# Inverse query norms written to DRAM word by word, and another place for one attention chain

## The chip, the cores and the metric

The kernel runs on one core of a Trainium2 chip. The metric is the device time of one execution in microseconds (us). The kernel before took 2829.93 us, the median of three runs (2829.88 to 2833.13).

The engines are named as in the profile: PE multiplies matrices (PEld is its weight load), DVE is the vector engine, ACT the scalar engine, POOL the GpSimd engine, and SP issues every DMA of this kernel from one queue, in order. PSUM is the memory into which PE writes; SBUF holds the tiles; DRAM is outside.

## What is computed

A decoder trunk of two layers over 1024 positions and 1024 channels, in float32. Layer 0 is a gated delta rule with a feed-forward part and a gated per-layer embedding. From its result one shared K and V are projected. Layer 1 is stick-breaking attention over them with eight heads of 128 channels, then again a feed-forward part and an embedding. Only the attention is touched by the change:

```python
def sb_mixer(hn, k_sh, v_sh, w_q, q_norm, w_out):
    q = (hn @ w_q).reshape(b_, s_, SB_HEADS, SB_HEAD_DIM)
    q = (rms_norm(q, q_norm) * (SB_HEAD_DIM ** -0.5)).transpose(0, 2, 1, 3)
    o = stick_breaking(q, k_sh, v_sh)
    return o.transpose(0, 2, 1, 3).reshape(b_, s_, SB_WIDTH) @ w_out

# stick_breaking, for a block of queries t and all keys s < t:
    z = einsum('bhtd,bhsd->bhts', q, k)
    log_not = where(mask, log_sigmoid(-z), 0.0)
    suffix = cumsum(log_not, axis=3, reverse=True) - log_not
    wgt = exp(where(mask, log_sigmoid(z) + suffix, -inf))
    out = einsum('bhts,bhsd->bhtd', wgt, v)
```

The norm of a query is one number per position, 1/sqrt(mean(q*q) + eps). The kernel doesn't scale q by it; it scales the scores z instead.

## The kernel before

**One program, planned while it is built.** The work is written as many small generators. `Flow` (lines 83 to 257) keeps a model of the time of each engine and of the DMAs. At each point of its own clock it runs, among the generators that are ready, the one with the lowest key; among equal keys the one that was spawned first (line 233). Where none is ready it takes the next step of one long "fill", the dense products. The order in which generators issue instructions is the order in each engine's queue, and stays fixed when the program runs. All instructions pass through one helper, so the profile puts line 64 to all of them, and tiles are told apart by name. A `take` waits for a free buffer of a kind in the model, a `give` frees it. The model's prices (lines 114 to 221) fix the order only.

**The attention stage** (`attention`, line 1739) has two kinds of work. The dense part (`sb_dense`, line 1794) goes over the heads, and in each over K, V, Q of the first and then of the second half of the positions, 512 columns at a time. A dense product is 24 matmuls into an `mm` bank: every float32 product is made of three, of high and low parts (`mm3`, line 337). Then `sb_features` (line 1817) splits the result into high and low parts for the attention. For Q and K it also transposes it, sums the squares of each position on ACT into a `[128, 4]` tile (partition = position within 128, column = which 128), and takes the power -0.5 on POOL.

For K this tile, `rk`, is used as it is, one number per partition. For Q the numbers are needed along the columns of z, the same in all partitions. So the tile goes through DRAM: PE transposes it into a `z` bank, DVE copies the `[4, 128]` result into `rr`, SP writes that to the DRAM tensor `rD`, and SP loads it back as one row of 512 numbers, repeated over 128 partitions (`rw`). The load waits for the write to have landed.

**The chains.** For each head h and half T, `sb_chains(h, T)` (line 1875) spawns three generators: `front` (key 2), `back` (key 0) and `out` (key 1). They go over the blocks of 128 keys from the last one backwards: four blocks for T = 0, eight for T = 1, of which the first four cover 128, 256, 384 and 512 columns. A front waits until the features of its head and half are there, and takes one of two `c` accumulator banks, which the back gives free at its last block. For each block: three matmuls make z; DVE scales it by `rk` and `rw` (tile `zs`); three ACT functions and a DVE one make the softplus (tile `t`); POOL masks the diagonal block; DVE splits it into `sh` and `sl`; four matmuls with triangles accumulate the suffix in `c`; DVE subtracts it from `zs`; POOL masks; ACT takes the exponential; DVE splits it into `wh` and `wl`; three matmuls with V accumulate the output in `o`. There are 4 `zs`, 2 `t`, 4 `sh`, 4 `sl`, 2 `wh`, 2 `wl` tiles, and 2 `z` banks for chains and features together.

**The end of the stage.** When the dense part is done, the fill goes on with `out_first` (line 1221), the output projection of the first half. Its first two units, f = 0 and 1, are made together: heads k = 0 to 6 of both, then k = 7 of both, which needs the output of chain (7,0). When its tile `x` exists, a chain's output is copied and split straight into it by ACT and DVE (`spill`, line 1184); before that it goes to DRAM (`oD`) and is loaded back (`load_o`, line 1206). The projection of the second half comes in the next stage, `tail(1)`, and needs chain (7,1).

All chains are spawned at the start of the stage, in the order (0,0), (0,1), (1,0), ... (6,1), (7,0), (7,1). So where two chains ask for the same thing at the same moment, the earlier one of this list gets it.

Of the kernel before, what the change touches and what calls it, by code (L numbers as in the profile page):

```python
# [15 lines left out]
P = 128  # L16
# [3 lines left out]
H = 8  # L20
# [249 lines left out]
class Net:  # L270
# [1468 lines left out]
    def attention(self):  # L1739
        nc, io, tc, flow = self.nc, self.io, self.tc, self.flow  # L1740
        with ExitStack() as es:
            sp = es.enter_context(tc.tile_pool(name="as", bufs=2, reuse_waits="tile"))
            pp = es.enter_context(tc.tile_pool(name="ap", bufs=2, space=PSUM, reuse_waits="tile"))
            self.sp, self.pp, self.lead = sp, pp, 0.0
            self.banks = (pp, "c", 2)
            self.enames = ()
            self.kq = sp.tile([P, 1], F32, name="kq", bufs=1)
            nc.vector.tensor_scalar(self.kq, self.small[:, 1:2], self.small[:, 2:3], float(P) ** -0.5, op0=ALU.mult, op1=ALU.mult)
            self.junk = sp.tile([P, P], F32, name="ajunk", bufs=1)
            nc.scalar.preload_act_table_set("natural_log_exp_and_others")  # L1750
            self.ast = [{} for _ in range(H)]
            self.hdone = [0] * H

            def second():
                hs = {}

                def loads():
                    for k in range(NK):
                        yield from self.take("zs")
                        hs[k] = self.t(sp, "zs", bufs=4)  # L1760
                        nc.sync.dma_start(hs[k], self.hD[k][:, HW:])
                        flow.mark(("hs", k))
                        yield 0.7

                flow.spawn(loads(), 0)
                yield lambda: flow.done(("hs", 0))
                yield from self.normed(("n3", 1), self.r1, lambda k: hs[k], None, lambda: self.t(sp, "sh", bufs=4), "sh", lambda: self.give("zs"))

            flow.spawn(second(), 0)
            for h in range(H):  # L1770
                for T in range(2):
                    self.sb_chains(h, T)
            yield from self.sb_dense()
            flow.spawn(self.late(), 4)
            yield lambda: ("tile", ("ol", 1, 0)) in flow.at
            yield from self.out_first(1, self.hD, lambda: self.t(sp, "xt"))
            yield lambda: all(e in flow.at for e in ("loaded10", "loaded11", ("put", 1)))
            self.enames = ()
# [38 lines left out]
    def sb_features(self, n, h, hf, ps):  # L1817
        nc, sp, pp, flow, st = self.nc, self.sp, self.pp, self.flow, self.ast[h]
        yield from self.take("ev")
        yield  # L1820
        ev = self.t(sp, "ev")
        nc.scalar.copy(ev, ps)
        self.give("mm")
        a, b = (self.t(sp, n + p, dt=F32R, bufs=4 if n == "q" else 5) for p in "hl")
        st[n, hf] = (a, b)
        yield
        yield from self.take("z")
        pt = self.t(pp, "z")
        for c in range(4):
            nc.tensor.transpose(pt[:, c * P : (c + 1) * P], ev[:, c * P : (c + 1) * P], self.ident)  # L1830
        yield
        if n == "v":
            nc.scalar.copy(a, pt)
            yield
            nc.vector.tensor_tensor(b, pt, a.bitcast(F32), op=ALU.subtract)
            self.give("z", "ev")
            flow.mark(("ap", n, h, hf))
            return
        ms = self.t(sp, "ms" + n, (P, 4))
        for c in range(4):  # L1840
            nc.scalar.activation(self.junk, pt[:, c * P : (c + 1) * P], AF.Square, accum_out=ms[:, c : c + 1])
        self.give("z")
        src = ev
        if n == "k":
            nc.vector.tensor_scalar(ev, ev, self.kq, None, op0=ALU.mult)
        nc.vector.tensor_copy(a, ev)
        yield
        nc.vector.tensor_tensor(b, ev, a.bitcast(F32), op=ALU.subtract)
        yield
        self.give("ev")  # L1850
        nc.vector.tensor_scalar(ms, ms, 1.0 / P, EPS, op0=ALU.mult, op1=ALU.add)
        yield
        r = self.t(sp, "r" + n, (P, 4), bufs=4)
        nc.gpsimd.tensor_tensor(r, ms, self.nhalf[:, :4], op=ALU.pow)
        yield
        if n == "k":
            st["rk", hf] = r
            flow.mark(("ap", n, h, hf))
            return
        yield from self.take("z")  # L1860
        pr = self.t(pp, "z")
        nc.tensor.transpose(pr[:4, :P], r, self.ident)
        yield
        rr = self.t(sp, "rr", (4, P))
        nc.vector.tensor_copy(rr, pr[:4, :P])
        self.give("z")
        yield
        nc.sync.dma_start(self.rD[2 * h + hf], rr)
        yield
        rq = self.t(sp, "rw", bufs=3)  # L1870
        nc.sync.dma_start(rq, self.rD[2 * h + hf].rearrange("c p -> (c p)").unsqueeze(0).to_broadcast([P, HW]))
        st["rq", hf] = rq
        flow.mark(("ap", n, h, hf))
# [218 lines left out]
```

## Time and profile before

| what | value |
|---|---|
| median of three runs | 2829.93 us (2829.88 to 2833.13) |
| profiled execution, its own time | 2831.9 us |
| its span | 2830.2 us |
| PE busy | 2759.6 us (98%) |
| DVE busy | 2026.8 us (72%) |
| ACT busy | 1276.1 us (45%) |
| POOL busy | 881.6 us (31%) |
| writes `rD` | 16, of 2 KB, from 1537.8 to 1966.4 us |
| loads `rw` | 16, of 256 KB, from 1539.1 to 1967.6 us |
| SP's waits for a write `rD` to land | 18.7 us in 15 waits, longest 2.1 |

Times in rows count from the start of the span. A row of the instructions in order of time has start, length, engine, operation, out<-in, shapes, count, and in brackets the idle time of the engine before it with what ended it. Matmuls overlap, and their ends are modelled: the rate of PE is the distance between starts, not the length. "PEclk" is the clock that was granted, 1.00 for full speed. The attention stage runs from about 1537 to 2060 us of the span.

### The profile page before, as it was taken

The page shows a single profiled execution, that of the slowest core. Times are in us where ns is not written, and L with a number is a line of the kernel's source. Part 1 is how long each engine was busy: PE and PEld are TensorE (multiplying, and loading weights), DVE is VectorE, ACT ScalarE, POOL GpSimd, SP SyncE. Part 2 cuts the span into 40 slices and gives each one's busy share as a digit, 9 for nine tenths or more (in the row PEclk, how much of TensorE's full clock was granted, in tenths as well). Part 3 has the DMA queues.
Part 4 walks back from the last instruction along what each step waited for, and adds up shares of the span by engine and source line. Part 5 has one row for each costly group of instructions (what it writes and reads, how often), then busy time and mean ns, then how long its engine had stood idle before and what let it go on. Part 6 is the DMA issues. An engine that isn't in the chain of part 4 may idle for free.

```text
span 2830.2 us, 37782 instructions
## 1 busy us (share of the span) xinstructions
PE 2759.6 (98%) x13203; PEld 2271.2 (80%) x13203; DVE 2026.8 (72%) x3861; ACT 1276.1 (45%) x2567; POOL 881.6 (31%) x742
## 2 busy tenths in 40 slices
PE   8899999999999999999999999999999999999999
PEld 7687777888878888888877778887777888888777
DVE  7777787784685655477867888998796655557783
ACT  6646545553443433322345566666453333422241
POOL 0101110110056666543201222221027666734400
PEclk9999999999999999999999999999999999999999
DMA  4312221227624444587432111114524444477622
GB/s 144 130 60 78 68 73 63 77 84 247 218 79 157 145 151 149 198 313 305 152 129 95 49 46 64 60 46 160 178 91 143 155 143 155 152 287 284 266 97 104
DMA packets 165631, 395.89 MB, mean 140 GB/s; under 512 B 34048, under 2 KB 35392, under 8 KB 155968
## 3 DMA queue, kind: packets, MB, share of 16 engines
q1 hardware_dynamic: 165440, 393.48, 39.1%
q8 instruction: 104, 1.70, 0.3%
q14 instruction: 87, 0.71, 0.1%
HBM read 274.29 MB, written 119.11 MB: 139 GB/s over the span
## 4 chain that ended last, share of the span: by engine, by line
PE 74%; DVE 14%; ACT 2%; issue 2%; DMA 2%; POOL 1%; SPq 0%; POOLq 0%; DVEq 0%; ACTq 0%
PE dn L64 37%; PE mm L64 27%; PE tp L64 3%; PE z L64 2%; PE c L64 2%; PE o L64 2%; DVE yr L64 1%; DVE x L64 1%; DVE ca L64 1%; DVE wlo L64 1%; DVE xr L64 1%; DVE u L64 1%; DVE v L64 1%; DVE hx L64 1%; PE po L64 1%
## 5 line engine op out<-in xcount | busy, mean ns | idle before, releaser
L64 PE MATMUL mm<-x,whi 128*128 128x512 f32 x2880 | 951.2, 400 | 12.8 <-DVE x L64 7.9
L64 PEld LDWEIGHTS mm<-x,whi 128*128 128x128 f32 x2880 | 533.6, 189 | 115.0 <-DVE x L64 13.8
L64 PE MATMUL mm<-x,wlo 128*128 128x512 f32 x1440 | 573.7, 398 | 0.0
L64 PE MATMUL dn<-x,whi 128*128 128x512 f32 x1776 | 549.2, 390 | 2.1 <-DVE x L64 0.9
L64 POOL TENSOR_TENSOR wlo<-raw,whi 128x512 fp32r<-128x512 f32 x236 | 346.0, 1487 | 442.0 <-ACT whi L64 368.1
L64 ACT CAST whi<-raw 128x1024 fp32r<-128x1024 f32 x231 | 242.9, 1052 | 445.3 <-DVE raw L64 258.4
L64 PEld LDWEIGHTS dn<-x,whi 128*128 128x128 f32 x1776 | 333.1, 188 | 74.7 <-DVE x L64 3.3
L64 PE MATMUL dn<-x,wlo 128*128 128x512 f32 x888 | 345.8, 389 | 0.0
L64 PEld LDWEIGHTS mm<-x,wlo 128*128 128x128 f32 x1440 | 271.6, 189 | 47.5 <-issue 0.2
L64 PE MATMUL dn<-hx,whi 128*128 128x512 f32 x864 | 267.6, 391 | 0.5 <-DVE hx L64 0.4
L64 DVE TENSOR_TENSOR tt<-u,tt 128x512 fp32r<-128x512 f32 x140 | 144.4, 1031 | 82.0 <-ACT tt L64 82.0
L64 PEld LDWEIGHTS dn<-x,wlo 128*128 128x128 f32 x888 | 166.7, 188 | 34.4
L64 PEld LDWEIGHTS dn<-hx,whi 128*128 128x128 f32 x864 | 162.8, 189 | 35.5 <-DVE hx L64 1.3
L64 DVE TENSOR_TENSOR v<-v,dn 128x512 f32<-128x512 f32 x112 | 76.6, 685 | 155.2 <-PE dn L64 154.6
L64 DVE TENSOR_TENSOR wlo<-raw,whi 128x512 fp32r<-128x512 f32 x226 | 155.5, 698 | 33.9 <-ACT whi L64 33.8
L64 PE MATMUL dn<-hx,wlo 128*128 128x512 f32 x432 | 169.2, 392 | 3.4 <-POOL wlo L64 3.4
L64 POOL TENSOR_TENSOR wlo<-sw,whi 128x512 fp32r<-128x512 f32 x102 | 144.4, 1433 | 0.8 <-ACT whi L64 0.8
L64 ACT CAST tt<-u 128x512 fp32r<-128x512 f32 x140 | 85.1, 620 | 125.4 <-DMA yD<-tt 102.3
L64 DVE TENSOR_TENSOR E<-E,dn 128x512 f32<-128x512 f32 x132 | 90.0, 684 | 69.2 <-PE dn L64 66.9
L64 POOL TENSOR_TENSOR rs<-ms,nhalf 128x4 f32<-128x4 f32 x11 | 12.4, 1123 | 330.0 <-DVE ms L64 260.5
L64 DVE SCALAR_TENSOR_TENSOR ca<-xe,conv,ca 128x512 f32<-128x512 f32 x144 | 107.6, 749 | 6.2 <-ACT ca L64 6.0
L64 PE MATMUL dn<-y,whi 128*128 128x512 f32 x352 | 108.4, 389 | 0.0
(333 smaller groups left out, 5136.5 us busy)
## 6 DMA issues: line engine op xcount, KB each, us to landing
yD<-tt SPq DMA_DIRECT2D x296, 256.0 KB
x<-yD SPq DMA_DIRECT2D x58, 1024.0 KB
raw<-f_s SPq DMA_DIRECT2D x84, 512.0 KB
raw<-d_s SPq DMA_DIRECT2D x40, 512.0 KB
raw<-w_in SPq DMA_DIRECT2D x33, 512.0 KB
hx<-yD SPq DMA_DIRECT2D x16, 1024.0 KB
x<-oD SPq DMA_DIRECT2D x27, 512.0 KB
raw<-g_out SPq DMA_DIRECT2D x16, 512.0 KB
```

What stands on the lines that cost most here:

```text
L64: r = issue(*args, **kw)
```

## The change

Two edits.

In `sb_features`, the transpose of the inverse query norms, the DVE copy of its result, the `z` bank that they used and the tile `rr` are gone. The DMA writes straight from the `[128, 4]` tile `r` into the same place of `rD`, seen with its two dimensions swapped: the word of partition p and column c goes to place 128 c + p. The load behind it is as before.

In `attention`, two chains are spawned in another order: (7,0) now comes ahead of (6,1). (7,1) stays last.

```diff
             flow.spawn(second(), 0)
-            for h in range(H):
-                for T in range(2):
-                    self.sb_chains(h, T)
+            chains = [(h, T) for h in range(H) for T in range(2)]
+            for h, T in chains[:-3] + [chains[-2], chains[-3], chains[-1]]:
+                self.sb_chains(h, T)
             yield from self.sb_dense()
...
             st["rk", hf] = r
             flow.mark(("ap", n, h, hf))
             return
-        yield from self.take("z")
-        pr = self.t(pp, "z")
-        nc.tensor.transpose(pr[:4, :P], r, self.ident)
-        yield
-        rr = self.t(sp, "rr", (4, P))
-        nc.vector.tensor_copy(rr, pr[:4, :P])
-        self.give("z")
-        yield
-        nc.sync.dma_start(self.rD[2 * h + hf], rr)
+        nc.sync.dma_start(self.rD[2 * h + hf].rearrange("c p -> p c"), r)
         yield
         rq = self.t(sp, "rw", bufs=3)
```

## The prediction

> **What bounds the kernel now.** I read the page first, then the busy time by stretches of the attention stage, the PE's instructions in order of time, and the SP's and DVE's around each inverse norm.
>
> ```profile
> span 2830.2 us, 37782 instructions
> PE 2759.6 (98%) x13203; PEld 2271.2 (80%) x13203; DVE 2026.8 (72%) x3861; ACT 1276.1 (45%) x2567; POOL 881.6 (31%) x742
> PE 74%; DVE 14%; ACT 2%; issue 2%; DMA 2%; POOL 1%; SPq 0%; POOLq 0%; DVEq 0%; ACTq 0%
> ```
>
> PE is the bound: 74% of the chain that ended last is PE. A change is worth the PE time it removes and the PE idle time it fills or opens. The diff touches only the attention stage, so I cut that into stretches (start:end, length, then busy us and count for PE, PEld, DVE, ACT, POOL, the granted clock, DMA share, GB/s).
>
> ```profile
> 1540.00:1700.00 160.00, 154.58 (x755) 127.65 (x754) 131.06 (x285) 97.38 (x247) 40.74 (x53) 0.98 0.15 53
> 1700.00:1920.00 220.00, 219.94 (x1097) 182.97 (x1095) 200.85 (x434) 151.27 (x368) 57.39 (x77) 1.00 0.16 56
> 1976.10:1986.70 10.60, 7.75 (x33) 4.90 (x32) 9.53 (x25) 6.24 (x15) 1.76 (x5) 1.00 0.02 9
> 1986.70:2060.00 73.30, 73.30 (x325) 60.12 (x325) 53.33 (x93) 35.52 (x52) 1.80 (x5) 1.00 0.58 205
> ```
>
> From 1700 to 1920 PE has no idle time at all, and DVE is at 91%. PE idles in two places: the first heads (5.4 us of 160, with the clock at 0.98) and a hole at 1976, near the end of the stage.
>
> **The transpose and the copy.** Sixteen times (eight heads, two halves) a `[128, 4]` tile of inverse norms is transposed on PE, copied by DVE and written to DRAM; the change drops the first two. What a transpose costs PE is the spacing of its neighbours. A plain 512-column matmul takes 32.22 / 142 = 0.227 us.
>
> ```profile
> 1764.04 0.40 PE L64 MATMUL mm<-x,whi 128*128 128x512 f32 x1
> 1764.44 0.27 PE L64 MATMUL z<-cst,rq 128*4 128x128 f32 x1
> 1764.47 0.48 PE L64 MATMUL mm<-x,whi 128*128 128x512 f32 x1
> 1764.78 0.40 PE L64 MATMUL mm<-x,wlo 128*128 128x512 f32 x1
> 2029.11 32.22 PE mm L64 x142
> ```
>
> From 1764.04 to 1764.78 PE spends 0.74 us where two matmuls need 0.45: 0.29 us for a transpose in a first half of the rows. In a second half the delay ahead of it is gone (0.03 + 0.31 - 0.227 = 0.11 us by the same spacing). Eight of each: 8 x 0.29 + 8 x 0.11 = **3.2 us**, lower bound 16 x 0.11 = 1.8. PE time in a PE-bound stretch is time of the kernel. The 16 DVE copies (0.27 us each, 4.3 us) count for nothing by themselves, since PE covers them.
>
> PE also waits for the POOL power that makes the inverse norm, since the transpose stands in PE's own queue:
>
> ```profile
> PE z L64 <- POOL rq L64: 4.1, 4, 2.1
> 1609.79 3.79 POOL L64 TENSOR_TENSOR rq<-msq,nhalf 128x4 f32<-128x4 f32 x1 [5.41 <-DVE msq L64]
> 1706.01 1.07 POOL L64 TENSOR_TENSOR rq<-msq,nhalf 128x4 f32<-128x4 f32 x1 [2.04 <-ACT t L64]
> 1613.63 0.27 PE L64 MATMUL z<-cst,rq 128*4 128x128 f32 x1 [2.08 <-POOL rq L64]
> 1615.53 0.63 PE L64 MATMUL o<-wh,vh 128*128 128x512 f32 x1
> 1615.96 0.63 PE L64 MATMUL o<-wl,vh 128*128 128x512 f32 x1
> 1679.12 0.27 PE L64 MATMUL z<-cst,rq 128*4 128x128 f32 x1 [1.44 <-POOL rq L64]
> 1613.87 0.42 ACT L64 ACTIVATE zs<-zs 128x256 f32<-128x256 f32 x1 [2.71 <-POOL zs L64]
> ```
>
> A power that mostly takes 1.07 us took 3.79 at 1609.79, and PE stood 2.08 us. After that stop matmuls came every 0.43 us (1615.53 to 1615.96) instead of 0.227, for about ten of them: 10 x 0.2 = 2.0 us more. The waits (4.1) and the slow matmuls (2.0) make 6.1 us that can go. But the slow power stays on POOL, and what is queued behind it there, a mask of the weights, made ACT wait 2.71 us in the same place; PE would have met that delay a few matmuls later. Ends: 0.6 (the two short waits) and 6.1. I take **3.5**, about the middle, because DVE and ACT have been seen to pass such a delay on.
>
> **The write, word by word.** Each row of four words per partition now goes to a `[4, 128]` place in DRAM with its words 512 bytes apart: 512 pieces of 4 bytes where there were 4 of 512. No row shows 4-byte writes. The load `rw` behind it stands in SP's queue and waits for the landing; behind it wait the next weight loads and spills.
>
> ```profile
> 1707.77 0.26 SPq L64 DMA_DIRECT2D rD<-rr  x1
> 1708.94 0.34 SPq L64 DMA_DIRECT2D rw<-rD  x1
> 1765.07 0.26 SPq L64 DMA_DIRECT2D rD<-rr  x1
> q1 hardware_dynamic: 1095, 0.16, 31.7%
> q1 hardware_dynamic: 144, 0.26, 21.1%
> 1709.50:1712.50 3.00, 3.00 (x15) 2.42 (x14) 2.97 (x7) 2.85 (x11) 0.00 (x0) 1.00 0.32 93
> 1712.50:1713.77 1.27, 1.27 (x9) 1.19 (x8) 1.27 (x3) 1.24 (x3) 0.69 (x1) 1.00 0.00 0
> 1746.00:1749.85 3.85, 3.85 (x22) 3.15 (x21) 3.85 (x9) 2.69 (x5) 1.96 (x2) 1.00 0.00 0
> ```
>
> Today write to load is 1.17 us. The fourth row is the DMA queue from 85.5 to 88.6, where four stores of 128-byte pieces ran: 31.7% of 16 engines for 3.1 us over 1095 packets, 14.4 ns each. The fifth is 1708.9 to 1713, the `rw` load in 2 KB pieces: 0.211 x 16 x 4.1 / 144 = 96 ns each. With 32 words per engine the write is longer by 32 x 14.4 = 0.46 us at the least and 32 x 96 = 3.07 at the most, landing after 1.6 to 4.2 us. A word is nearer to 128 bytes than to 2 KB, so I take about 1.7. Against that, the write can start as soon as the power is done: 1706.01 + 1.07 = 1707.08, 0.7 us earlier. The last rows give the slack: the `rw` data are in by 1712.5, and the first DVE instruction of the chain that reads them starts at 1713.77 (first half); in a second half, in by 1746.0 and read at 1749.85. So 1.3 and 3.9 us. At the value taken the load is late by 0.5 - 0.7, which is not late: **0**. The planner, whose prices set the order only, charges the write 0.73 us more (line 199 multiplies its bytes by 128) and no longer counts a bank, a transpose and a copy ahead of it, so I take the places of `rw` and of the chain as unchanged. At the upper end it is late by 3.07 - 0.7 - 1.3 = 1.1 us in seven first halves; DVE, at 91%, can't hide that: up to 7.7 us lost.
>
> The page "DMA: Bandwidth & Descriptors" of the Trainium skill speaks against this edit (Rules for kernel authors): a strided last dimension becomes one descriptor per element, and it sets a rearranged plain DMA 19 times behind the hardware's transpose. By 19 times the present 1.17 us the write would take an estimated 22 us; no run here shows a write of that kind.
>
> **The order of the chains.** Chain (7,0) is now spawned ahead of (6,1), so it wins whenever both ask for the same buffer or engine. The rest of `sb_dense` and of the first two output units is used up at 1976.10, and their last product (k = 7) needs (7,0)'s output. Rows: the last and the first dense matmul around the hole, its first and last of 25 groups, and the DVE scaling of the first and last block of (0,0), which ran alone, and of (7,0).
>
> ```profile
> 1976.10 0.39 PE L64 MATMUL mm<-x,wlo 128*128 128x512 f32 x1
> 1986.71 0.44 PE L64 MATMUL mm<-x,whi 128*128 128x512 f32 x1
> L64 PE MATMUL o<-wh,vl 128*128 128x512 f32 x3 | 1.2, 391 | 0.0
> L64 PE MATMUL z<-qh,kh 128*128 128x128 f32 x1 | 0.2, 222 | 0.0
> 1543.61 0.35 DVE L64 SCALAR_TENSOR_TENSOR zs<-z,rk,rw 128x128 f32<-128x128 f32 x1 [0.89 <-issue]
> 1556.54 0.75 DVE L64 SCALAR_TENSOR_TENSOR zs<-z,rk,rw 128x512 f32<-128x512 f32 x1
> 1949.60 0.35 DVE L64 SCALAR_TENSOR_TENSOR zs<-z,rk,rw 128x128 f32<-128x128 f32 x1
> 1973.40 0.75 DVE L64 SCALAR_TENSOR_TENSOR zs<-z,rk,rw 128x512 f32<-128x512 f32 x1
> ```
>
> The hole holds 33 matmuls: 12 of 512 columns, 6 of 384, 5 of 256, 10 of 128; at 0.227 us per 512 columns that is 4.9 us of work in 10.6, so 5.7 us lost (busy time, 7.75, hides it, as ends are modelled). Alone, a chain of this length needs 12.9 us from first to last block; (7,0) took 23.8. With right of way it can come up to 10.9 us earlier, the length of the hole. Since (6,1) still has blocks in flight I count on 8 of 10.6: 5.7 x 8 / 10.6 = 4.3, and the dense work at hand fills the rest with what the chains leave: **4.5**. Ends: 0 and 5.7. What is late next is (6,1), by as much; its output is wanted by the next stage's projection, which needs (7,1) too, and that chain follows later still. (7,1) gets the accumulator bank that (7,0) frees earlier. So no new wait there. The swap moves the chain's matmuls, DVE, ACT and POOL instructions by priority alone; its loads stand in `sb_features`, and its output goes by ACT and DVE copies into `x`, as today, so no DMA is moved past another on SP.
>
> **Sum.** 3.2 + 3.5 + 0 + 4.5 = 11.2 us. The profiled execution took 2831.9 us (span 2830.2 and 1.7 around it): 2820.7. It was 2.0 above the median of the runs, 2829.93, so the median comes to 2818.7, say **2819**. With all ends against it: 1.8 + 0.6 + 0 - 7.7, a loss of 5.3; with all for it 3.2 + 6.1 + 5.7 = 15.0.
>
> **Rivals.**
>
> *The hole stays.* The planner decides from its own times, and (7,0) may still come last. Only 6.7 us remain: 2823. For: the slots of a chain are given in order of asking; against: the planner picks by spawn order among those ready.
>
> *Words land at the upper end* (4.2 us): 11.2 - 7.7 = 3.5, 2826. For: words of different partitions, written by different engines, lie side by side in the same 2 KB; against: so do the 128-byte pieces, at 14.4 ns.
>
> *The words go one after another* instead of over 16 engines: 512 x 14.4 ns = 7.4 us more. Place: DVE's scaling at the start of each chain, late by 7.4 - 0.7 - 1.3 = 5.4 us in first halves, 2.8 in second. DVE's spare time is 9% of a head (57 us, 5.2), so 8.2 - 5.2 = 3 to 8.2 us a head, plus slow matmuls after each stop (2.0, twice): 3 to 12, middle 7.5; over seven heads 52 less 11: 2870, **slower**. It decides once the landing takes about 5 us, where the loss of 1.6 us a head eats the gain. The 19 times of the page would end here and beyond.
>
> *POOL's power falls badly in the new order*, again and again, since the heads repeat:
>
> ```profile
> 1655.40 3.12 POOL L64 TENSOR_TENSOR rk<-msk,nhalf 128x4 f32<-128x4 f32 x1 [0.68 <-DVE msk L64]
> 1660.35 0.50 PE L64 MATMUL z<-qh,kh 128*128 128x512 f32 x1 [1.48 <-DVE zs L64]
> ```
>
> Here the power of the keys took 3.12 us and PE stood 1.48; with slow matmuls some 3.5 us. In all five repeating heads 17.5 us, less 11.2: 2836. Against: today those heads show none.
>
> *The change doesn't act*: stops move elsewhere and the swap meets an order that was the same already: 2829.
>
> **Chances.** Forecast 0.55 (2813 to 2824); hole stays 0.15; upper end 0.12; serial words 0.06; POOL 0.05; no action 0.07. A measurement here tells about 0.2% (5.7 us) from no change: faster means under 2824.3. That takes the forecast but for 0.02 of it and 0.09 of the first rival: 0.62; slower is serial words and POOL, 0.11; the same 0.27. The range, from a gain of 18 (all ends, and the stop at 1660 gone) to 2832 (a little past the no-action case), leaves out the slower cases and some overshoot.
>
> **What would show it.** No PE wait for the power of the queries; about 0.4 us less per head from 1700 on (57.3 between the `rD` writes of two heads now, 1707.77 to 1765.07); write to load 1.6 to 2 us; no DVE wait for `rw`; dense matmuls right through the former hole, and (7,0)'s last block before (6,1)'s. DVE idle ahead of `zs` ended by the `rw` load, or write to load over 5 us, would make the prediction wrong.

## The result and the profile after

The changed kernel takes **2903.36 us**, the median of four runs (2902.23 to 2905.91); the kernel before took 2831.53 beside it. The ratio is 1.0252, interval 1.0237 to 1.0267: 2.5% slower, where a gain of 0.4% was forecast and 2832 was the upper end of the range. No ratio here counts one execution of 13540 us, which stands far above all others of its kernel (the one with the earlier row, below).

First the page of the profile after: the span, the busy time of the engines, the shares of the chain that ended last, and from the costliest groups the scaling of the scores.

```profile
span 2901.7 us, 37715 instructions
PE 2780.9 (96%) x13187; PEld 2286.2 (79%) x13187; DVE 2027.1 (70%) x3845; ACT 1278.0 (44%) x2567; POOL 877.3 (30%) x742
PE 66%; DVE 14%; DMA 8%; issue 3%; ACT 3%; POOL 1%; SPq 0%; DVEq 0%; POOLq 0%; ACTq 0%
L64 DVE SCALAR_TENSOR_TENSOR zs<-z,rk,rw 128x128 f32<-128x128 f32 (+3 forms) x96 | 58.9, 614 | 80.5 <-DMA rw<-rD 69.5
```

DMA now holds 8% of the chain (2% before), and DVE stands 69.5 us ahead of the scaling, for the row `rw`. PE has 16 instructions less, yet it is busy 21.3 us longer (2780.9 less 2759.6) and idle 50.2 us longer (120.8 now, 70.6 before, span less busy). Together that is the whole difference of the spans, 71.5. The idle time is in the attention stage, where the clock has fallen too (columns as in the prediction):

```profile
1540.00:1700.00 160.00, 135.47 (x627) 111.63 (x626) 107.66 (x231) 80.69 (x207) 29.76 (x45) 0.91 0.14 45
1700.00:1920.00 220.00, 201.63 (x949) 165.82 (x948) 174.72 (x373) 130.67 (x317) 50.93 (x66) 0.95 0.22 47
```

One stop, from its cause to its end: SP's queue, then DVE's, then PE's instructions of the same 16 us.

```profile
1731.84 0.37 SPq L64 DMA_DIRECT2D rD<-rq  x1
1740.14 0.32 SPq L64 DMA_DIRECT2D rw<-rD  x1
```

```profile
1737.22 0.69 DVE L64 TENSOR_TENSOR kl<-ev,kh 128x512 fp32r<-128x512 f32 x1
1745.03 0.35 DVE L64 SCALAR_TENSOR_TENSOR zs<-z,rk,rw 128x128 f32<-128x128 f32 x1 [7.11 <-DMA rw<-rD]
```

```profile
1739.81 0.39 PE L64 MATMUL mm<-x,wlo 128*128 128x512 f32 x1
1746.37 0.69 PE L64 MATMUL o<-wh,vh 128*128 128x384 f32 x1 [6.18 <-DVE wh L64]
1748.63 0.63 PE L64 MATMUL z<-qh,kh 128*128 128x512 f32 x1
1749.05 0.63 PE L64 MATMUL z<-ql,kh 128*128 128x512 f32 x1
```

The write takes 8.30 us from its issue to the issue of the load behind it, which waits for it to land; it was 1.17. (Over all sixteen writes it is 7.5 to 11.3 us.) DVE reaches the scaling of a new chain and stands 7.11 us. Behind that instruction, in the same queue, are the splits of the chain before, which need nothing of the row; PE waits for one of them, `wh`, for 6.18 us. Then its 512-column matmuls start 0.42 us apart (1748.63 to 1749.05), not 0.227: that is the longer busy time. The waits of the stage show the same from above (waited in all, times, longest):

```profile
DVE zs L64 <- DMA rw<-rD: 69.5, 13, 8.8
ACT t L64 <- DVE zs L64: 125.8, 45, 10.4
PE z L64 <- ACT ev L64: 18.7, 4, 7.5
PE c L64 <- DVE sl L64: 14.7, 4, 6.5
PE o L64 <- DVE wh L64: 11.2, 3, 6.2
```

What the write does in its 8.3 us is in the view of the DMA engines from 1598.8 to 1607.3, around another of the sixteen (busy tenths in 40 slices of 0.21 us, then packets, MB and share of 16 engines, then the issue):

```profile
DMA  0000271000000000000000001000000000000000
q1 hardware_dynamic: 528, 0.00, 3.0%
rD<-rq SPq DMA_DIRECT2D x1, 2.0 KB, 8.3
```

528 packets took 3.0% of 16 x 8.5 us, 4.1 us of engine time or 7.7 ns each, and they were through some 1.5 us after the issue (slice 7). The landing came 8.3 us after it. So the DMA engines were not busy with the words for most of that time; the landing itself was late.

### The profile page after: what moved, and what is told of

Same layout as the page of the kernel before. It is cut to its first block, busy times and chain, and to the rows that moved or that the text cites. A ratio compares the mean times of both kernels' runs of the same rounds, so it can differ in the third digit from the quotient of the medians.

```text
span 2901.7 us, 37715 instructions
## 1 busy us (share of the span) xinstructions
PE 2780.9 (96%) x13187; PEld 2286.2 (79%) x13187; DVE 2027.1 (70%) x3845; ACT 1278.0 (44%) x2567; POOL 877.3 (30%) x742
## 4 chain that ended last, share of the span: by engine, by line
PE 66%; DVE 14%; DMA 8%; issue 3%; ACT 3%; POOL 1%; SPq 0%; DVEq 0%; POOLq 0%; ACTq 0%
PE dn L64 36%; PE mm L64 21%; DMA rD<-rq 4%; PE tp L64 2%; DMA rw<-rD 2%; DVE yr L64 2%; PE z L64 2%; PE c L64 1%; DVE x L64 1%; PE o L64 1%; DVE xr L64 1%; DVE ca L64 1%; DVE wlo L64 1%; DVE u L64 1%; DMA Ls<-Ld 1%
## 5 line engine op out<-in xcount | busy, mean ns | idle before, releaser
L64 PE MATMUL mm<-x,whi 128*128 128x512 f32 x2880 | 961.2, 404 | 13.0 <-DVE x L64 8.1
L64 PEld LDWEIGHTS mm<-x,whi 128*128 128x128 f32 x2880 | 540.3, 191 | 117.7 <-DVE x L64 14.1
L64 DVE SCALAR_TENSOR_TENSOR zs<-z,rk,rw 128x128 f32<-128x128 f32 (+3 forms) x96 | 58.9, 614 | 80.5 <-DMA rw<-rD 69.5
## 6 DMA issues: line engine op xcount, KB each, us to landing
x<-yD SPq DMA_DIRECT2D x58, 1024.0 KB, 10.5
```

The source lines that it names most:

```text
L64: r = issue(*args, **kw)
```

## The experiments

The numbers are medians beside 2832 to 2833 for the kernel before in the same comparison. Ratios are to the kernel before.

**Each edit alone.** First only the order of the chains:

```diff
-            for h in range(H):
-                for T in range(2):
-                    self.sb_chains(h, T)
+            chains = [(h, T) for h in range(H) for T in range(2)]
+            for h, T in chains[:-3] + [chains[-2], chains[-3], chains[-1]]:
+                self.sb_chains(h, T)
```

> Only the chains' order is changed; the transpose, the copy and the write in four rows of 512 bytes stay. If the loss is the landing of the word-wise write: a gain of about 4.5 us (ratio 0.998), the hole at the end of the stage mostly filled, write to load 1.2 us. If the loss came from the new place of the chain: a good part of the 72 us, ratio about 1.02.

2834.74 us, ratio 1.0007 (0.9998 to 1.0016): nothing gained. The last dense matmul ahead of the hole and the first behind it:

```profile
1978.37 0.40 PE L64 MATMUL mm<-x,wlo 128*128 128x512 f32 x1
1989.35 1.05 PE L64 MATMUL mm<-x,whi 128*128 128x512 f32 x2
```

11.0 us; the hole was 10.6. The chain that was to come earlier, (7,0), did not start earlier: its write and its first scaling on DVE are 12.3 us apart, as before (1937.31 to 1949.60). The rows are its write, then its first and its last scaling.

```profile
1939.87 0.27 SPq L64 DMA_DIRECT2D rD<-rr  x1
```

```profile
1952.15 0.35 DVE L64 SCALAR_TENSOR_TENSOR zs<-z,rk,rw 128x128 f32<-128x128 f32 x1
1971.34 0.73 DVE L64 SCALAR_TENSOR_TENSOR zs<-z,rk,rw 128x512 f32<-128x512 f32 x1
```

Behind its start the order did act. The last scaling comes 19.2 us after the first, where it was 23.8, and (7,0)'s output is now copied ahead of that of (6,1) (at 1986.10 and 1989.59; before, at 1984.45 behind 1982.03). But from the first scaling to the first dense matmul behind the hole it is 37.2 us, and it was 37.1: what the scalings gained was lost again between the last of them and the output. DVE was busy 13.0 of the 14 us from 1976 to 1990.

Then only the write, in the old order:

```diff
-        nc.tensor.transpose(pr[:4, :P], r, self.ident)
...
-        nc.vector.tensor_copy(rr, pr[:4, :P])
...
-        nc.sync.dma_start(self.rD[2 * h + hf], rr)
+        nc.sync.dma_start(self.rD[2 * h + hf].rearrange("c p -> p c"), r)
```

> Only the word-wise write; the chains stay in the old order. If the landing is the cause: write to load 8.2 us, DVE waiting about 70 us for the load, and a time some 70 to 78 us above the kernel before (ratio 1.025 to 1.028). If the order was the cause: near the kernel before.

2903.42, ratio 1.0255 (1.0241 to 1.0269), and the same wait:

```profile
DVE zs L64 <- DMA rw<-rD: 66.5, 13, 9.0
```

So the write is the whole loss.

**What makes it late.** The kernel before, with stores to fresh DRAM places after its end, each followed on SP by a small load that waits for the landing; three of each kind.

```diff
+    for i in range(3):
+        d = dr.tile(list(shape), F32, name=f"{tag}{i}")
+        nc.sync.dma_start(view(d), part)
+        nc.sync.dma_start(back[:1, :1], d[:1, :1])
```

> The kernel before, with stores of several shapes behind its end, each three times and one after another, each landing before the next. If the landing grows with the number of pieces: four rows of 512 bytes 1.2 us, 128 words 3, 256 words 5, 512 words 8, 128 pieces of 16 or 64 bytes 3 each, and 512 words far apart 8. If it is neighbouring words in the same place that hold each other up: 512 words 64 or 512 bytes apart land much earlier, about 2 us. If it is the size under 512 bytes alone: all but the rows land alike.

One of each of four kinds: four rows of 512 bytes; 512 neighbouring words; 128 neighbouring words; 512 words 64 bytes apart.

```profile
2839.88 0.21 SPq L2047 DMA_DIRECT2D pback<-rows  x1
...
2858.15 0.39 SPq L2046 DMA_DIRECT2D words<-psrc  x1
2866.52 0.21 SPq L2047 DMA_DIRECT2D pback<-words  x1
...
2914.76 0.35 SPq L2046 DMA_DIRECT2D quarterwords<-psrc  x1
2922.23 0.21 SPq L2047 DMA_DIRECT2D pback<-quarterwords  x1
...
2966.56 0.39 SPq L2046 DMA_DIRECT2D apart<-psrc  x1
2968.47 0.21 SPq L2047 DMA_DIRECT2D pback<-apart  x1
```

The rows took 1.20 us (issued at 2838.68), the words 8.4 to 9.7, a quarter of the words still 7.5 to 7.8, and the 512 words 64 bytes apart 1.8 to 2.1; 512 bytes apart gave the same, 1.8 to 2.0. Half the words took 7.9 to 8.1. The two kinds that lie apart have as many pieces, of the same size, as the words: **neither the number of pieces nor their four bytes cost the time, but that the words are neighbours in DRAM.** A second set of stores went through the distance between them:

```diff
+    probe("steptwo", (4 * P, 2), lambda d: d.rearrange("(c p) w -> p c w", c=4)[:, :, 0], src)
+    probe("stepfour", (4 * P, 4), lambda d: d.rearrange("(c p) w -> p c w", c=4)[:, :, 0], src)
+    probe("stepeight", (4 * P, 8), lambda d: d.rearrange("(c p) w -> p c w", c=4)[:, :, 0], src)
```

> The kernel before, with more stores behind its end. If writes into the same 64 bytes go one after another: 512 words at steps of 8, 16 and 32 bytes land after about half, a quarter and an eighth of the extra 7 us of words side by side (4.7, 3 and 2.1 us), and pieces of 8 bytes like words at steps of 8. If only neighbours within the same 32 bytes or within one engine's share matter, the 32-byte step lands in 2 us and the others near 8.

```profile
2877.77 0.38 SPq L2046 DMA_DIRECT2D steptwo<-psrc  x1
2882.05 0.21 SPq L2047 DMA_DIRECT2D pback<-steptwo  x1
...
2893.41 0.38 SPq L2046 DMA_DIRECT2D stepfour<-psrc  x1
2896.12 0.21 SPq L2047 DMA_DIRECT2D pback<-stepfour  x1
```

| 512 words, distance of one from the next | issue to the load behind it |
|---|---|
| 4 bytes | 8.5 to 9.7 us |
| 8 bytes | 3.2 to 4.3 |
| 16 bytes | 2.7 to 2.8 |
| 32 bytes | 2.0 to 2.1 |
| 64 bytes (set before) | 1.8 to 2.1 |

Neighbouring pieces of 8 bytes (256, two per partition) took 3.2 to 4.1; those of 16 bytes (128, one per partition) 1.5 to 2.8; those of 32 and 64 bytes 1.5. Both sets read as if words within a stretch of some tens of bytes were written one after another, and different stretches side by side: 128 neighbouring words, with as many words per stretch as 512, take nearly as long. One kind doesn't fit that: 128 words at steps of 16 bytes took 1.5, where 512 at the same steps took 2.7. So the picture is not complete, and why the landing is late no run here shows.

**How the late row becomes 72 us.** The changed kernel as it is, but the planner, which sets the order only, is told that this write lands after 8.3 us:

```diff
             end = self.rings
+            if outs[0].space == DRAM and outs[0].shape[-1] == 4:
+                end = t + 8.3
```

> The changed kernel, but the planner's price for the word-wise write is 8.3 us, as measured, instead of 1.8; nothing else. If the loss comes from DVE's queue, in which scaling instructions stand that were planned 6 us too early: DVE's 69 us of waiting for the load mostly go and the time falls by over 50 us, to within 15 of the kernel before. If a chain can't be filled by other work while it waits (lateness itself is the price): the idle time moves to PE with other names and the time stays over 2880.

2847.19, ratio 1.0060 (1.0040 to 1.0079):

```profile
DVE zs L64 <- DMA rw<-rD: 20.3, 9, 4.9
```

The write is as slow as before (8.4 to 11.8 us), SP's queue is held as long by the load behind it, and yet 56 of the 72 us are back. So most of the loss was not the lateness of the row, nor the time for which SP's queue is held. It lay in the order of queues that are fixed in advance, DVE's above all, which held instructions that need the row ahead of others that don't.

Another way to give the write time is to compute the queries earlier: from the second head on, the product for Q comes ahead of that for V (the weights are loaded in that order too), in the old order of chains.

```diff
-            for n, hf in (("k", 0), ("v", 0), ("q", 0), ("k", 1), ("v", 1), ("q", 1)):
+            for n, hf in [(n, hf) for hf in range(2) for n in ("kqv" if h else "kvq")]:
```

> The word-wise write, the old order of the chains, but from the second head on the product for Q comes ahead of that for V (24 matmuls, 5.4 us), so that the write has one product more to land in before the chain starts. Theory (the loss is DVE's scaling planned some 6 us before the words are in): DVE's wait for the row falls from 66 us to under 20, and the time from 2903 to 2830 to 2850. Rival (SP's queue, held 8 us a time by the load behind the write, delays weights and spills): 2880 or more, whatever DVE waits for.

2899.66, ratio 1.0235 (1.0217 to 1.0252): a miss by 50 us. One stop of it, SP's queue and then DVE's:

```profile
1653.17 0.37 SPq L64 DMA_DIRECT2D rD<-rq  x1
1663.70 0.32 SPq L64 DMA_DIRECT2D rw<-rD  x1
```

```profile
1659.02 0.69 DVE L64 TENSOR_TENSOR vl<-z,vh 128x512 fp32r<-128x512 f32 x1
1660.28 0.54 DVE L64 TENSOR_TENSOR zs<-zs,c 128x384 f32<-128x384 f32 x1
1667.55 0.35 DVE L64 SCALAR_TENSOR_TENSOR zs<-z,rk,rw 128x128 f32<-128x128 f32 x1 [6.72 <-DMA rw<-rD]
```

DVE's wait for the row did not fall: 65.8 us in 11 waits. The features of V (`vl`) come only some 6 us after the write's issue, and the chain right behind them; and the landing grew to 10.5 us. It is 10 to 12 us in most of this kernel's writes that have a spill or a weight load in flight, and 8 to 9.5 where nothing is. The delay goes the other way too: in the changed kernel three weight loads were issued within 1 us behind such a write, and they landed after 11.4 to 12.1 us, where the median of these loads is 3.6. What that costs, and what SP's queue costs, the rival named there, was not separated from DVE's wait. Only the first of the two ways helped.

**A write that doesn't have the trouble.** Four words of a partition can be written as one piece of 16 bytes, in the order (p c), but then the row in DRAM is in another order than the columns of z. Three kernels, all in the old order of the chains, deal with that differently. In the first, DVE reads the row in steps of four words (the scaling's other arguments are left out here):

```diff
+        nc.sync.dma_start(self.rD[2 * h + hf].rearrange("c p -> (c p)").rearrange("(p c) -> p c", c=4), r)
...
-                nc.vector.scalar_tensor_tensor(..., rq[:, cols], ...)
+                nc.vector.scalar_tensor_tensor(..., rq.rearrange("q (p c) -> q c p", c=4)[:, 4 - n // P :], ...)
```

> The old order of the chains, no transpose and no copy, but the tile is written as it lies, 128 pieces of 16 bytes, and DVE reads the row in steps of four numbers instead of one. If the landing grows with the number of pieces: about 1.2 + 7.1 x 128 / 512 = 3 us, little or no DVE wait for the load, and a time 3 to 8 us below the kernel before. If any write of pieces under 512 bytes lands late: 8 us again, and about 70 us above it. If the strided read slows DVE: the scaling of 512 columns takes more than 0.75 us.

2842.48, ratio 1.0035 (1.0021 to 1.0049). The wait is gone (1.5 us in one), but the scaling itself became longer; here its 512-column form:

```profile
L64 DVE SCALAR_TENSOR_TENSOR zs<-z,rk,rw 128x512 f32<-128x512 f32 x48 | 53.8, 1121 | 3.4 <-PE z L64 3.4
```

Before it was 744 ns (48 x 0.377 = 18 us more of DVE). To see what the write alone is worth, the second kernel leaves the reordering out, so the scores are scaled with the norms of other positions:

> Old order of the chains; no transpose and no copy; the tile is written as it lies, 128 pieces of 16 bytes, and read back in that order without any reordering, so the scores are scaled by the inverse norms of other positions. This is the change with its slow write taken away and nothing put in its place. If the two terms of the prediction for the transposes and for PE's waits hold: 3 to 9 us below the kernel before (ratio 0.997 to 0.999), no PE wait for the power of the queries. If the stalls only move: the same time within 3 us.

2821.69, ratio 0.9959 (0.9947 to 0.9972): 11.2 us faster, more than the 3 to 9 expected. The third does the reordering with an ACT copy after the load:

> As the kernel with the 16-byte pieces and the old order, but ACT puts the row back in order, one copy of 512 columns per head and half, so that DVE reads it in unit steps. If the strided read by DVE was what that kernel lost by: its 10 us go, and with the transposes gone the time comes 0 to 6 us below the kernel before. If the ACT copy delays the chains or takes over 1 us each: no gain.

2859.71, ratio 1.0095 (1.0081 to 1.0109): 27 us slower than the kernel before. ACT's queue now waits for the row, and each copy takes 1.12 us. Besides, the load of the last row was issued only 26.8 us after its write, behind other transfers in SP's queue. How the loss divides between these is not shown.

```profile
ACT rw L64 <- DMA xt<-rD: 22.4, 8, 4.2
```

**The version that keeps the gain.** The order can be changed for nothing where the squares are made: the transposed Q is used for its squares only, so the transposes may take every fourth column.

```diff
-            nc.tensor.transpose(pt[:, c * P : (c + 1) * P], ev[:, c * P : (c + 1) * P], self.ident)
+            nc.tensor.transpose(pt[:, c * P : (c + 1) * P], ev.rearrange("d (p c) -> d c p", c=4)[:, c] if n == "q" else ev[:, c * P : (c + 1) * P], self.ident)
```

> The write in 16-byte pieces again (four neighbouring words of one partition), the old order of the chains, but the four transposes of Q in front of the squares now take every fourth column, so that partition p holds positions 4p to 4p+3 and the row in DRAM comes out in the right order; nothing has to be reordered behind it and the result is the whole one. Theory (what was lost is the landing of neighbouring words; the removed transpose and PE's wait for the power are worth 11 us): 2821 to 2823 against 2832 before, as with the row left unordered. Rival (PE's reading with a step of 16 bytes is slow): 64 transposes of 128 columns; if each takes 0.11 us more, 7 us are lost again and it ends at 2829.

2821.83, ratio **0.9966** (0.9953 to 0.9979): 0.3% faster than the kernel before, with the whole result.

```profile
span 2820.1 us, 37731 instructions
PE 2755.6 (98%) x13187; PEld 2271.1 (81%) x13187; DVE 2020.9 (72%) x3845; ACT 1273.9 (45%) x2567; POOL 882.2 (31%) x742
```

```profile
1540.00:1700.00 160.00, 159.68 (x796) 133.63 (x796) 136.84 (x298) 104.66 (x264) 40.30 (x59) 1.00 0.20 57
1700.00:1920.00 220.00, 218.91 (x1079) 181.69 (x1078) 198.84 (x422) 146.99 (x358) 56.67 (x73) 1.00 0.19 54
```

PE is busy 4.0 us less and idle 6.1 less than before. In the first heads its idle time went from 5.4 us to 0.3 and the clock from 0.98 to 1.00. The write takes 1.4 to 3.1 us, and DVE waits for the row 2.7 us in all.

**Which part of that gain is PE's wait for the power?** The kernel before, with the power priced at 3.8 us in the planner during the attention stage, so that the transposes are put later:

```diff
-            return 0.295 + 0.166 * n if kw.get("op") == ALU.pow else ...
+            return (3.8 if self.dear and n == 4 else 0.295 + 0.166 * n) if kw.get("op") == ALU.pow else ...
```

`dear` is true from the start of the attention stage to its end.

> The kernel before, transposes and all, but the planner's price of the power on [128, 4] in the attention stage is 3.8 us instead of 0.96, the longest that the trace shows, so that the transposes are put later in PE's queue. Nothing else. Theory (PE's waits for the power, 4.1 us, and the slow matmuls behind the longest, 2.0, are time of the kernel): no PE wait for the power, 2825 to 2828 against 2832. Rival (the wait goes to whoever comes next, chains that start later): 2831 to 2836. If it gains as much as the 16-byte write without transposes (11 us), the transposes' own time counted for nothing.

2836.21, ratio 1.0014 (1.0004 to 1.0024). No PE wait for the power of the queries is left in its trace, but nothing is gained, as the rival had it: what needs the row is put later too (the last write `rD` starts 437.1 us after the first, instead of 428.5). Moving the transpose away from the wait is not enough; the gain came where the transpose went. What the wait alone is worth this run doesn't show, since it delays the rows as well.

**Why the order gained nothing.** With the landing mended and the new order together:

> As the kernel whose Q transposes take every fourth column (16-byte write, 2821.8), and with the new order of the chains, (7,0) ahead of (6,1): the whole change, with the landing of its write mended. Theory (DVE, not the right of way, sets the end of (7,0); the order alone gave 1.0007 of the kernel before): 2820 to 2824, no difference to 2821.8. Rival (the order could show nothing before because the stage ahead of it was later in that run): 2817 or less.

2824.45, ratio 0.9966 (0.9952 to 0.9979), the same as with the old order. There the hole is nearly gone anyway (3.9 us in the old order, 2.7 in the new), and (7,0) is ahead of (6,1) without the new order: in the old one its last scaling stands at 1958.73, that of (6,1) at 1961.06. One more cause was open: in the kernel before, the row of (7,0) stood in SP's queue behind a weight load that waited for a free buffer.

```profile
1937.31 0.27 SPq L64 DMA_DIRECT2D rD<-rr  x1
1937.63 0.87 SPq L64 DMA_DIRECT2D x<-oD  x2
1942.82 0.35 SPq L64 DMA_DIRECT2D raw<-s_out  x1
1943.27 0.38 SPq L64 DMA_DIRECT2D rw<-rD  x1
```

So the kernel before, with those loads held back until that row is issued, in the old and in the new order:

```diff
             for key, src, _, _ in reqs:
                 yield lambda: count["load"] - count["split"] < 2
+                if key == ("o10", 0):
+                    yield lambda: ("ap", "q", H - 1, 0) in flow.at
```

> The kernel before with one edit: the loads of the output projection's weights don't start before the row of inverse norms of (7,0) is issued. Before, that row stood in SP's queue behind such a load, which waited for a free buffer: 5.96 us from the write to the row, where 1.2 is usual. Now the row goes ahead of the weights. Theory (the hole at 1976 comes from (7,0) starting late): the first scaling of (7,0) about 4 us earlier, the hole (10.6 us, 5.7 lost) half as long, 2827 to 2830 against 2832.5. Rival (DVE, 9.5 us busy in the 10.6 of the hole, sets the end of (7,0) whenever it starts): 2831 to 2835.

> The same with the change's order of the chains, (7,0) ahead of (6,1). Theory that a late start took the effect from the order: with the row in time the right of way counts, 2822 to 2828, at least 3 us less than with the old order. Rival (the order is worth nothing either way): within 2 us of the same kernel with the old order.

2837.04, ratio 1.0009 (0.9998 to 1.0021) in the old order; 2830.64, ratio 0.9990 (0.9981 to 0.9999) in the new one. The dense matmuls around the hole, first with the old order, then with the new:

```profile
1983.25 0.40 PE L64 MATMUL mm<-x,wlo 128*128 128x512 f32 x1
1992.61 0.73 PE L64 MATMUL mm<-x,whi 128*128 128x512 f32 x1
```

```profile
1976.69 0.40 PE L64 MATMUL mm<-x,wlo 128*128 128x512 f32 x1
1983.20 0.82 PE L64 MATMUL mm<-x,whi 128*128 128x512 f32 x2
```

The row's load now comes 3.4 and 2.6 us after its write, and (7,0)'s first scaling 10.0 us after it in both. The earlier row alone leaves the hole at 9.4 us and the time where it was or a little above; with the new order it is 6.5 us, and the two ratios differ by 0.0019, some 5 us (execution by execution, a mean of 2835.6 in ten against 2830.5 in eleven). That is what was expected of a right of way that counts once the row is in time, though the level is above the expected 2822 to 2828 and the two intervals still overlap by 0.0001. Against the kernel before, row and order together are 0.1% faster; in the kernels with the mended write the order showed nothing, and in the change as made it was worth nothing.

## Why the prediction was wrong

**The write** is the step that failed. It was sized by the time of packets on the 16 engines (14.4 to 96 ns each) and put at a landing of 1.7 us, 4.2 at most. The packets were even cheaper than that, 7.7 ns, and were through after some 1.5 us; but the landing was 8.3. The bounds came from a row of stores in 128-byte pieces and one of a load in 2 KB pieces. Neither has pieces that share a small stretch of DRAM, and both give the time of packets, which does not bound the landing. The argument against the upper end, that the 128-byte pieces also lie side by side, compared the wrong distance: what counts lies at a few tens of bytes.

The rule of the Trainium skill that the prediction set beside this, in the page "DMA: Bandwidth & Descriptors" (Rules for kernel authors), pointed the right way: one descriptor per element agrees with the 528 packets, and the time is 7 times the 1.17 us of the rows, not the 19 times taken from it. The number of descriptors isn't what cost here, though: as many words 64 bytes apart landed in 1.9 us.

**The slack** of 1.3 us in first halves was about right, if a little long. With a landing 7.1 us later, DVE waited 6.2 us in the mean of the eight first halves and 2.5 in that of the second (69.5 us in all); the rival "words go one after another" had 5.4 and 2.8.

**That rival**, at 0.06, had the place and the size (7.4 us more, 7.1 measured), but not the mechanism, so its size came by luck. It let the packets go one after another at 14.4 ns each. By that, 128 words would have landed 1.8 us later than rows and 512 words 64 bytes apart 7.4; they landed 6.3 to 6.6 and 0.6 to 0.9 us later. Its time of 2870 was too low: it let DVE's spare time take up part of each stop, and took the middle of 3 to 12 us a head. Against the kernel with the mended write, the loss is (2903.4 - 2821.8) / 8 = 10.2 a head, near its upper end. DVE's spare time helps little when DVE's queue itself is held, as the kernel whose planner knew the landing shows, and slow matmuls came behind the stops (a granted clock of 0.91 from 1540 to 1700, where it was 0.98).

**The transposes and the wait for the power**, 3.2 + 3.5 = 6.7 us, had the right sign and were too small together: 10.7 with the mended write. PE's busy time fell by 4.0 us there, which fits the transposes and slow matmuls that are gone. The wait was cut from 6.1 to 3.5 because POOL's slow power was thought to stop PE again later; PE's idle time in the first heads fell by 5.1. How the 10.7 divide between these two and the smaller hole isn't settled: the one run that took the wait away alone gained nothing.

**The order of the chains**, 4.5 us, failed as a step: nothing came (1.0007), as in the rival "the hole stays". But that rival had the planner leave (7,0) last, and it did not. The 12.9 us from first to last scaling of a chain that ran alone were taken for what right of way gives. It gave 19.2 instead of 23.8, and the output came no earlier: the sum left out the path behind the last scaling. Two things in the trace of before spoke against it: (7,0)'s row was held in SP's queue, so that it could not start earlier, and DVE, which all chains share, was busy 9.53 of the hole's 10.60 us. The hole did shrink where the row came in time (6.5 us with the new order, 3.9 in the kernel with the mended write and the old order), so DVE's work is not the whole of it; how much each holds isn't settled.

The rivals of POOL's power and of a change without effect did not show: PE has no wait for the power of the queries after the change, and none that is put down to POOL, though four powers still took 2.5 to 3.3 us.

## What to carry to other kernels

Bound a store by when it lands, not by its packets: pieces that are small and neighbours in DRAM, from different partitions, should be made wide enough (here 16 bytes) or be ordered at their source, where a transpose can permute for nothing. Where queues are fixed in advance, price a new transfer in the planner before judging it: beside the kernel with the mended write, the same late write cost 82 us when it was planned as early and 25 when it was planned as late. A free place in a queue is not the same as an idle engine; before counting on right of way, look at how busy the engine is that all contenders share.

## What the runs showed of the hardware

- 512 words of 4 bytes from 128 partitions to neighbouring places in DRAM landed 8.4 to 9.7 us after their issue, 128 such words 7.5 to 7.8, and the same 512 words at 64 bytes from each other 1.8 to 2.1.
- DVE's scaling of 512 columns took 1121 ns with its second input read in steps of 16 bytes, 744 ns with neighbouring words. PE's weight load for a transpose with the same step cost little: the 180 loads of the stage, 64 of them strided, took 162 ns in the mean instead of 140, and the transposes 278 instead of 273.
- Weight loads of 512 KB issued within 1 us behind a write of 512 neighbouring words landed after 11.4 to 12.1 us, where the median of these loads is 3.6; with the write in 16-byte pieces none took over 6.0.
- After a stop of 6.18 us PE's 512-column matmuls started 0.42 us apart until about 1752, some 6 us, and then 0.23 apart.
